# A Mamba-2 scan woven into matmul products: TensorE's instructions in traced order, the mask applied late, loads two steps ahead

## The chip, the cores and the metric

The kernel runs on one core of a Trainium2 chip. The metric is the device time of one launch in microseconds, as the median of the runs; a run is also profiled, and the profile gives every instruction of every engine with start and duration.

## What is computed

The reference is one decoder block: an RMSNorm, a wide projection `n @ w_in`, a Mamba-2 branch (SSD) and a gated linear attention branch (GLA) on parts of it, a gated merge, cross-attention to a short memory, and a SwiGLU feed-forward, all in float32 with 1024 tokens and 1024 features. The change lies in the SSD branch, which is, cut to what matters:

```python
xBC = silu(causal_dwconv(xBC, conv_w, conv_b))          # conv over tokens, then Silu
xs, Bm, Cm = split(xBC, [1024, 1024 + 2 * 128], axis=-1)
X = x_heads * dt[..., None]; a_cs = cumsum(dt * A)       # per chunk
CB = einsum('bclgn,bcsgn->bcgls', Cc, Bc)
y_diag = einsum('bcgls,bgrcls,bcsgrp->bclgrp', CB, segsum_exp(a), X)
states = einsum('bclgn,bgrcl,bclgrp->bcgrpn', Bc, exp(a_cs[..., -1:] - a_cs), X)
# state of a chunk = state before * exp(a_cs[..., -1]) + states
y_off = einsum('bclgn,bcgrpn,bgrcl->bclgrp', Cc, prev_state, exp(a_cs))
y = (y_diag + y_off + D * x_heads) * silu(z)
y = rmsnorm over each group's 512 features
```

There are 16 heads of 64 features in two groups, and a state of 128. The kernel uses chunks of 128 tokens, so there are 8 chunks x 2 groups = 16 items.

## The kernel before, in words

The projection is computed in units of 256 output columns. A unit (`Unit`, line 273) is one level of a seven-product scheme: its products B11, T2, T1, B21, T3, B22, T4 (this order is `SPACED`, line 40, and holds for a unit that runs alone) are each 12 matmuls of 128 x 128 by 128 x 512 into one PSUM bank. For each product, ScalarE makes the high part `whi` of the weights, VectorE the rest `wlo`, and VectorE or ScalarE evacuates the bank into `o`; GpSimd or VectorE makes the sums and differences of weights (`sa`, `raw`). These side instructions are traced with a priority 200 ahead of their place.

The kernel is written for a scheduler. The Python program traces instructions in one order; the scheduler then puts each engine's instructions in an order of its own, by priority and by when a model of the chip says that their inputs are ready. On the chip each engine runs its own list in that fixed order and waits on semaphores.

Ahead of the stage in question, six units (`xu`) project the channels of the convolution. `conv(u, unit)` (line 723) runs one unit behind: ScalarE starts a block `cv` of 128 channels, VectorE adds three taps, ScalarE applies Silu, and SP stores the block to `xbc_d` in DRAM. Unit 5 holds the rows of C (two blocks, one for each group). Its convolution is traced whole after the last unit's products and before the stage in question.

The stage in question then runs nine units (`ru`, `qk`, the first of `gs`), 63 products, and `run` (line 436) weaves the SSD steps between them: after each product it adds a rate to a counter, and for each whole number in it the generator `ssd_steps` is advanced to its next `yield`, with a priority of `PRIO` = 1000 ahead. Before the change the rate is 64/63, and what is left over is traced after the 63 products.

An item (class `SSD`, line 870) has these parts:

- `load`: SP loads the item's x channels and z gate (`xz`), B and C (`bc`), and a broadcast of the cumulated decay (`csb` from `cs_d`).
- `lay`: TensorE multiplies B and C (`bank<-bc`) and transposes B and the x channels into two banks; VectorE masks CB with a triangle (`cbm`), ScalarE copies B's transpose (`bt`), VectorE scales x by dt (`xd`).
- `decay`: ScalarE makes `e` (eight Relus with a bias, one Exp) and the Exp of `csb`; GpSimd makes `xc`; VectorE multiplies `csb` by C and `e` by the masked CB.
- `scan`: TensorE's 16 + 16 small products (`bank<-e,xd`, `bank<-csb,state`) and the state's products (`bank<-xc,bt`); GpSimd and VectorE update the state.
- `gate`: VectorE, GpSimd and ScalarE make `y` and the sum of its squares, `rd`.
- `stat`: a matmul sums `rd` over partitions, VectorE and GpSimd make the inverse root `rs`.
- `norm`: a matmul spreads `rs`, VectorE scales `y`, SP stores it to `ys_d`.

PSUM has four banks (`bank`) for these and four (`acc`) for the products. The SSD buffers (`xz` 3, `bc` 2, `csb` 2, `e` 2, `xc` 1) lie where the convolution's buffers lay.

Of the kernel before, what the change touches and what calls it, by code (L numbers as in the profile page):

```python
# [9 lines left out]
F32 = mybir.dt.float32  # L10
# [6 lines left out]
P = 128  # L17
# [11 lines left out]
CH = 128  # L29
NCH = TOK // CH  # L30
NH = 16
GH = 8
# [3 lines left out]
PRIO = 1000  # L36
# [42 lines left out]
def block_kernel(ctx: ExitStack, tc: tile.TileContext, t: dict, out: bass.AP):  # L79
    nc = tc.nc  # L80
    now = [0.0]
    PE, ACT, SP = Tensor(nc.tensor, now), nc.scalar, nc.sync
    DVE, POOL = Meter(nc.vector, now, 0.06, 1.04e-3), Meter(nc.gpsimd, now, 0.08, 2.25e-3)
# [6 lines left out]
    def pool(name, bufs=1, space=None, stack=None):  # L90
        kw = {"reuse_waits": "tile"} if space is None else {"space": space}
        return (stack or ctx).enter_context(tc.tile_pool(name=name, bufs=bufs, **kw))
# [6 lines left out]
    def dram(name, *shape):  # L99
        return dr.tile(list(shape), F32, name=name, tag=name)  # L100
# [4 lines left out]
    xbc_d = dram("xbc_d", 1536, TOK)  # L105
    sz_d = dram("sz_d", D, TOK)
# [18 lines left out]
    def bank(dt=F32):  # L125
        return ps.tile([P, 512], dt, name="bank", tag="bank", bufs=4)
# [3 lines left out]
    mul = lambda e, o, a, b: e.tensor_tensor(o, a, b, ALU.mult)  # L130
# [35 lines left out]
    triu = cp.tile([P, P], F32, name="triu")  # L166
# [106 lines left out]
    class Unit:  # L273
# [10 lines left out]
        def load(s):  # L284
            if s.raw is None:
                s.raw = slot(s.key, (P, 2 * s.kh, 256), name="raw")
                SP.dma_start(s.raw, s.W[s.row0:s.row0 + 256 * s.kh, s.c0:s.c0 + 256].rearrange("(k p) c -> p k c", p=P))
# [124 lines left out]
    def group(units, B, then=(), nxt=None, frm=6, products=7):  # L412


        for u in units:
            u.load()
        then = list(then)
        many = len(units)
        for n, name in enumerate((CHAIN if many > 1 else SPACED)[:products]):
            for x, u in enumerate(units):  # L420
                u.step(name, B)
                if many > 1:
                    B.upto((n + 1) * B.kh - (-(x + 1) * B.kh // many))
                if n == 6 and nxt:
                    nxt.upto((x + 1) * nxt.kh // many)
                if n >= frm and then:
                    then.pop(0).load()
                while len(posts) > lag[0]:
                    settle()
                    if n < 4:  # L430
                        break
                yield
        for u in then:
            u.load()

    def run(main, *rest, prio=0):

        owed = [0.0] * len(rest)
        for _ in main:
            for i, (g, rate) in enumerate(rest):  # L440
                owed[i] += rate
                while owed[i] >= 1.0:
                    owed[i] -= 1.0
                    with tc.high_priority(offset=prio):
                        next(g, None)
# [5 lines left out]
    def drain(g):  # L451
        for _ in g:
            pass

    def singles(units, B, then=()):

        for u, nxt in zip(units, list(units[1:]) + [None]):
            yield from group([u], B, [nxt] if nxt else then)

    def store_rows(dst, func=None):  # L460

        def mk(base):
            def post(i, j, ap):
                if func is not None:
                    ACT.activation(ap, ap, func)
                SP.dma_start(dst[base + i * P:base + (i + 1) * P, half(j)], ap)
            return post
        return mk

    def w_in_units(c0, n, mk):  # L470
        return [Unit(t["w_in"], 0, c0 + 256 * u, post=mk(256 * u)) for u in range(n)]
# [64 lines left out]
    for k in range(NB):  # L536
        p = bank()
# [73 lines left out]
    B = Operands(hb, 4)  # L611
# [230 lines left out]
    ru = w_in_units(R0, 4, store_rows(sr_d))  # L842
    qk = w_in_units(Q0, 2, store_rows(q_d)) + w_in_units(K0, 2, store_rows(k_d))
    gs = w_in_units(GS0, 4, store_rows(gs_d))
# [18 lines left out]
    sp_ = pool("ssd", 1, stack=st3)  # L863
# [6 lines left out]
    class SSD:  # L870
# [8 lines left out]
        def load(s):  # L879
            g, tk = s.g, s.tk  # L880
            s.L = sp_.tile([P, 8, CH], F32, name="xz", tag="xz", bufs=3)
            SP.dma_start(s.L[:, 0:4], xbc_d[g * 512:(g + 1) * 512, tk].rearrange("(k p) s -> p k s", p=P))
            s.BC = sp_.tile([P, 2, CH], F32, name="bc", tag="bc", bufs=2)
            for i in range(2):
                r0 = 1024 + i * 256 + g * P
                SP.dma_start(s.BC[:, i], xbc_d[r0:r0 + P, tk])
            s.csb = sp_.tile([P, GH, CH], F32, name="csb", tag="csb", bufs=2)
            SP.dma_start(s.csb.rearrange("p h s -> p (h s)"),
                         cs_d[s.i0:s.i0 + GH, :].rearrange("h s -> (h s)").partition_broadcast(P))
            SP.dma_start(s.L[:, 4:8], sz_d[g * 512:(g + 1) * 512, tk].rearrange("(k p) s -> p k s", p=P))  # L890

        def lay(s):
            p = bank()
            PE.matmul(p[:, :P], s.BC[:, 0], s.BC[:, 1], start=True, stop=True)
            PE.transpose(p[:, P:2 * P], s.BC[:, 0], ident)
            s.cbm = sp_.tile([P, CH], F32, name="cbm", tag="cbm", bufs=2)
            mul(DVE, s.cbm, p[:, :P], triu)
            s.bt = sp_.tile([P, P], F32, name="bt", tag="bt", bufs=2)
            ACT.activation(s.bt, p[:, P:2 * P], AF.Copy)
            p = bank()  # L900
            for k in range(4):
                PE.transpose(p[:, k * P:(k + 1) * P], s.L[:, k], ident)
            s.xd = sp_.tile([P, GH, 64], F32, name="xd", tag="xd", bufs=2)
            mul(DVE, s.xd, p.rearrange("p (h d) -> p h d", d=64), s.heads(dt_h, 64))

        def decay(s):
            s.e = sp_.tile([P, GH, CH], F32, name="e", tag="e", bufs=2)
            for h in range(GH):
                ACT.activation(s.e[:, h], s.csb[:, h], AF.Relu, bias=cs[:, s.i0 + h:s.i0 + h + 1], scale=-1.0)  # L909
            ACT.activation(s.e, s.e, AF.Exp, scale=-1.0)  # L910
            ACT.activation(s.csb, s.csb, AF.Exp)
            s.xc = sp_.tile([P, GH, 64], F32, name="xc", tag="xc", bufs=1)
            mul(POOL, s.xc, s.xd, s.heads(dec, 64))
            mul(DVE, s.csb, s.csb, s.BC[:, 1].unsqueeze(1).to_broadcast([P, GH, CH]))
            mul(DVE, s.e, s.e, s.cbm.unsqueeze(1).to_broadcast([P, GH, CH]))

        def scan(s):
            st = state[s.g]
# [37 lines left out]

    def ssd_steps():
        it = [SSD(c, g) for c in range(NCH) for g in range(2)]
        it[0].load()
        yield  # L960
        it[0].lay()
        yield
        it[0].decay()
        yield
        for i in range(len(it) + 1):
            z = it[i - 1] if i else None
            a = it[i] if i < len(it) else None
            b = it[i + 1] if i + 1 < len(it) else None
            if b:
                b.load()  # L970
            if a:
                a.scan()
            yield
            if z:
                z.stat()
            if b:
                b.lay()
            yield
            if a:
                a.gate()  # L980
            yield
            if z:
                z.norm()
            if b:
                b.decay()
            yield

    ssd = ssd_steps()
    run(singles(ru + qk + gs[:1], B, gs[1:2]), (ssd, 16 * 4 / 63), prio=PRIO)
    drain(ssd)  # L990
    st3.close()

# [426 lines left out]
    for n in range(len(at) + 2):  # L1419
        a = at[n] if n < len(at) else None  # L1420
        b = at[n - 1] if 0 < n <= len(at) else None
        z = at[n - 2] if n > 1 else None
# [59 lines left out]
    B = Operands(b_xo, 4, order=("B11", "T1", "B21", "B22", "T2", "T3", "T4"))  # L1482
# [147 lines left out]
    for x, (n, k, kn) in enumerate(todo):  # L1630
        name = CHAIN[n]
# [58 lines left out]
```

## Time and profile before

| what | value |
|---|---|
| median of 3 runs (1959.33 to 1963.98) | 1959.69 us |
| the profiled execution: time, span of the trace | 1964.03 us, 1962.3 us |
| mean granted clock of TensorE | 0.996 |
| DMA | 317.98 MB, 162 GB/s over the span |
| `wlo<-raw,whi` on VectorE, stage of SSD and GLA | x75, mean 881 ns |
| `o<-acc,o` on VectorE, the same | x74, mean 683 ns |
| `cbm<-bank,triu` on VectorE | x16, median 275 ns |
| `rs<-bank` on VectorE; `rs<-rs,mhalf` on GpSimd | median 145 ns; mean 1041 ns |
| ScalarE's idle time before `e<-csb,cs`, until `csb` landed | 17.4 us, 11 times |

The profile calls the engines PE (TensorE's matmuls), PEld (its weight loads), DVE (VectorE), ACT (ScalarE), POOL (GpSimd) and SP (the queue that issues the DMAs). Matmuls overlap in the records: one lasts 389 ns in the mean, though in a full stream one starts every 0.227 us, so busy time alone hides short waits. `L51` is the line of a helper that records every matmul and `L73` that of one which records every VectorE and GpSimd instruction, so groups are told apart by the names of their tiles: `acc<-T2h,whi` is a matmul of a product, `bank<-bc` the first of an item's `lay`.

### The profile page before, as it was taken

Reading aid. Unit: us, or ns where it says so; the run is one execution under the profiler, and the core shown is the slowest. Engines: PE = TensorE matmul, PEld = TensorE weight load, DVE = VectorE, ACT = ScalarE, POOL = GpSimd, SP = SyncE. Lnnn points to the kernel's source line nnn. Section 1 sums busy time; section 2 is a strip of 40 time slices with the busy share of each in tenths; the row PEclk is TensorE's granted clock in tenths of the full one; section 3 lists DMA queues with packets and bytes.
Section 4 is the critical chain, followed back from the end, with each engine's and each line's share of the span. In section 5 each row is a group of like instructions: output and inputs, shape, how many; then the busy total and the mean of one; then the engine's idle time right before and its main releaser. Section 6 shows DMA issues by size and latency. Waiting matters only on the chain.

```text
span 1962.3 us, 26274 instructions
## 1 busy us (share of the span) xinstructions
PE 1921.4 (98%) x9772; PEld 1614.9 (82%) x9772; DVE 1315.5 (67%) x1851; ACT 848.2 (43%) x1492; POOL 595.7 (30%) x442
## 2 busy tenths in 40 slices
PE   8899999999999999999999999999999999999998
PEld 7898787878788888888888888878888888878887
DVE  6866779789886655565544246676777777774565
ACT  8434564465552554642223235453333333353243
POOL 1012334355553212113342000037444544320002
PEclk9999999999999999999999999999999999999999
DMA  9333373456544653997684101442242233176463
GB/s 314 140 120 100 124 285 108 149 182 197 167 155 134 204 161 104 355 365 260 244 290 152 47 22 44 145 134 81 92 133 99 81 110 132 62 276 209 160 225 120
DMA packets 238244, 317.98 MB, mean 162 GB/s; under 512 B 16907, under 2 KB 156405, under 8 KB 238117
## 3 DMA queue, kind: packets, MB, share of 16 engines
q1 hardware_dynamic: 238116, 316.31, 47.5%
q8 instruction: 77, 1.26, 0.3%
q14 instruction: 51, 0.41, 0.1%
HBM read 215.27 MB, written 100.99 MB: 161 GB/s over the span
## 4 chain that ended last, share of the span: by engine, by line
PE 76%; DVE 11%; issue 3%; DMA 3%; ACT 3%; POOL 2%; SPq 1%; POOLq 0%; DVEq 0%; ACTq 0%
PE acc L51 67%; PE bank L51 9%; DVE wlo L73 3%; DVE cv L73 2%; DVE o L73 2%; PE bank L55 1%; DMA csb<-cs_d 1%; DMA xt<-in_x_dram 1%; ACT e L909 1%; DVE hs L73 1%; DMA raw<-in_w_in_dram 1%; DMA fr<-act_d 1%; DVE fs L73 1%; POOL y L73 1%; POOL sa L73 0%
## 5 line engine op out<-in xcount | busy, mean ns | idle before, releaser
L51 PE MATMUL acc<-hl,wd 128*128 128x512 f32 x1920 | 438.7, 389 | 0.0
L51 PEld LDWEIGHTS acc<-hl,wd 128*128 128x128 f32 x1920 | 360.1, 188 | 74.3
L73 DVE TENSOR_TENSOR wlo<-raw,whi 128x512 fp32r<-128x512 f32 x272 | 245.4, 907 | 89.5 <-ACT whi L221 87.4
L221 ACT ACTIVATE whi<-raw 128x512 fp32r<-128x512 f32 x272 | 169.6, 628 | 238.5 <-PE acc L51 211.0
L73 DVE TENSOR_TENSOR o<-acc,o 128x512 f32<-128x512 f32 (+1 forms) x256 | 172.6, 676 | 115.8 <-PE acc L51 105.0
L73 POOL TENSOR_TENSOR sa<-raw 128x512 f32<-128x512 f32 x47 | 75.5, 1607 | 306.6 <-DMA raw<-in_w_ffn_in_dram 227.1
L51 PE MATMUL acc<-fs 128*128 128x512 f32 (+1 forms) x792 | 157.6, 358 | 2.2 <-ACT o L1585 2.0
L51 PEld LDWEIGHTS acc<-fs 128*128 128x128 f32 x792 | 131.8, 190 | 23.7 <-ACT o L1585 2.4
L73 POOL TENSOR_TENSOR raw<-raw,sa 128x512 f32<-128x512 f32 x48 | 68.7, 1431 | 242.8 <-DVE wlo L73 231.9
L221 ACT ACTIVATE fs<-fr 128x1024 fp32r<-128x1024 f32 (+1 forms) x84 | 80.0, 984 | 114.8 <-PE acc L51 40.5
L73 DVE TENSOR_TENSOR fs<-fr,fs 128x1024 fp32r<-128x1024 f32 (+1 forms) x84 | 99.7, 1218 | 40.5 <-ACT fs L221 40.1
L221 ACT ACTIVATE whi<-sa 128x512 fp32r<-128x512 f32 x96 | 60.0, 626 | 104.5 <-PE acc L51 101.4
L73 DVE TENSOR_TENSOR wlo<-sa,whi 128x512 fp32r<-128x512 f32 x96 | 82.9, 865 | 16.1 <-ACT whi L221 16.1
L73 DVE TENSOR_TENSOR wd<-raw,wd 128x1024 fp32r<-128x1024 f32 x40 | 53.3, 1334 | 48.5 <-ACT wd L221 48.4
L221 ACT ACTIVATE wd<-raw 128x1024 fp32r<-128x1024 f32 x40 | 42.2, 1059 | 96.0 <-PE acc L51 89.4
L73 POOL TENSOR_TENSOR raw<-raw 128x512 f32<-128x512 f32 x48 | 82.5, 1718 | 3.0 <-DVE sa L73 2.8
L51 PE MATMUL acc<-T4h,whi 128*128 128x512 f32 x192 | 75.9, 396 | 1.8 <-DVE o L73 1.8
L51 PE MATMUL acc<-B22h,wlo 128*128 128x512 f32 x192 | 76.2, 397 | 1.3 <-DVE wlo L73 1.3
L51 PE MATMUL acc<-B21h,whi 128*128 128x512 f32 x192 | 75.3, 392 | 1.4 <-ACT o L350 1.4
L51 PE MATMUL acc<-B21h,wlo 128*128 128x512 f32 x192 | 75.5, 393 | 0.4 <-DVE wlo L73 0.4
L51 PE MATMUL acc<-T3h,wlo 128*128 128x512 f32 x192 | 75.8, 395 | 0.0
L51 PE MATMUL acc<-B22h,whi 128*128 128x512 f32 x192 | 75.6, 394 | 0.0
(386 smaller groups left out, 4651.9 us busy)
## 6 DMA issues: line engine op xcount, KB each, us to landing
raw<-in_w_in_dram SPq DMA_DIRECT2D x26, 1024.0 KB, 5.7
raw<-in_w_ffn_in_dram SPq DMA_DIRECT2D x22, 1024.0 KB, 8.0
act_d<-o SPq DMA_DIRECT2D x77, 256.0 KB, 2.1
fr<-act_d SPq DMA_DIRECT2D x35, 512.0 KB, 6.0
pre<-in_w_ffn_out_dram SPq DMA_DIRECT2D x11, 1024.0 KB
fr<-down_d SPq DMA_DIRECT2D x20, 512.0 KB, 4.9
down_d<-pre SPq DMA_DIRECT2D x33, 256.0 KB, 3.5
raw<-in_w_xkv_dram SPq DMA_DIRECT2D x8, 1024.0 KB, 7.6
```

What stands on the lines that cost most here:

```text
L51: return s.e.matmul(o, x, y, **kw)
L55: return s.e.transpose(o, x, i)
L73: return f(*a, **kw)
L221: ACT.activation(hi, src, AF.Copy)
L909: ACT.activation(s.e[:, h], s.csb[:, h], AF.Relu, bias=cs[:, s.i0 + h:s.i0 + h + 1], scale=-1.0)
```

## The change

TensorE's instructions of the whole stage are put in the order in which they are traced, instead of the scheduler's order. The steps are dealt out anew, 74/63 to a product, so that all of them lie within the 63 products: with numbers for the steps of item i, step 1 has the `norm` of item i - 2 and the `scan` of item i; step 2 the `load` of item i + 2, the `stat` of item i - 1, the `lay` of item i + 1 and the `gate` of item i; step 3 the `decay` of item i + 1 and the load of `csb` for item i + 2; step 4 nothing. Ahead of them come the loads of two items after the first product, `lay` of item 0 after the second, its `decay` after the third, and its `scan` after the fourth. The mask is multiplied into CB in `decay`, with its result in the third quarter of CB's own bank, and the multiplication of `e` reads it there. B and C come with one DMA instead of two, into three buffers instead of two.

```diff
-            s.BC = sp_.tile([P, 2, CH], F32, name="bc", tag="bc", bufs=2)
-            for i in range(2):
-                r0 = 1024 + i * 256 + g * P
-                SP.dma_start(s.BC[:, i], xbc_d[r0:r0 + P, tk])
+            s.BC = sp_.tile([P, 2, CH], F32, name="bc", tag="bc", bufs=3)
+            SP.dma_start(s.BC, xbc_d[1024:1536, tk].rearrange("(i g p) s -> g p i s", g=2, p=P)[g])
+            SP.dma_start(s.L[:, 4:8], sz_d[g * 512:(g + 1) * 512, tk].rearrange("(k p) s -> p k s", p=P))
+
+        def load_cs(s):
             s.csb = sp_.tile([P, GH, CH], F32, name="csb", tag="csb", bufs=2)
             SP.dma_start(s.csb.rearrange("p h s -> p (h s)"), ...)
-            SP.dma_start(s.L[:, 4:8], sz_d[g * 512:(g + 1) * 512, tk].rearrange("(k p) s -> p k s", p=P))
...
-            p = bank()
+            p = s.p = bank()
...
-            s.cbm = sp_.tile([P, CH], F32, name="cbm", tag="cbm", bufs=2)
-            mul(DVE, s.cbm, p[:, :P], triu)
...
-            mul(DVE, s.e, s.e, s.cbm.unsqueeze(1).to_broadcast([P, GH, CH]))
+            cbm = s.p[:, 2 * P:3 * P]
+            mul(DVE, cbm, s.p[:, :P], triu)
+            mul(DVE, s.e, s.e, cbm.unsqueeze(1).to_broadcast([P, GH, CH]))
...
-        it[0].load()
+        n = len(it)
+        for s in it[:2]:
+            s.load()
+            s.load_cs()
         yield
         it[0].lay()
         yield
         it[0].decay()
         yield
-        for i in range(len(it) + 1):
-            z = it[i - 1] if i else None
-            a = it[i] if i < len(it) else None
-            b = it[i + 1] if i + 1 < len(it) else None
-            if b:
-                b.load()
+        for i in range(n + 2):
+            y, z, a, b, c = (it[k] if 0 <= k < n else None for k in range(i - 2, i + 3))
+            if y:
+                y.norm()
             if a:
                 a.scan()
             yield
+            if c:
+                c.load()
             if z:
                 z.stat()
             if b:
                 b.lay()
-            yield
             if a:
                 a.gate()
             yield
-            if z:
-                z.norm()
             if b:
                 b.decay()
-            yield
+            if c:
+                c.load_cs()
+            yield
+            if i < n:
+                yield
 
     ssd = ssd_steps()
-    run(singles(ru + qk + gs[:1], B, gs[1:2]), (ssd, 16 * 4 / 63), prio=PRIO)
+    with tc.manual_schedule(engines={mybir.EngineType.PE}):
+        run(singles(ru + qk + gs[:1], B, gs[1:2]), (ssd, 74 / 63), prio=PRIO)
     drain(ssd)
```

## The prediction

> **What bounds the kernel now.** I read the page first, then a table by stage, then the waits of TensorE inside the SSD stage.
>
> ```profile
> PE 1921.4 (98%) x9772; PEld 1614.9 (82%) x9772; DVE 1315.5 (67%) x1851; ACT 848.2 (43%) x1492; POOL 595.7 (30%) x442
> ```
> ```profile
> 380.00:593.00 213.00, 208.00 (x1320) 169.06 (x1320) 181.28 (x287) 117.36 (x257) 114.47 (x90) 1.00 0.58 178
> 593.00:787.00 194.00, 194.00 (x967) 163.96 (x967) 112.59 (x224) 83.30 (x198) 48.63 (x41) 1.00 0.49 153
> ```
>
> The columns of the second fence are the window, its length, busy time of PE, PEld, DVE, ACT and POOL, granted clock, DMA share, GB/s. TensorE bounds the kernel. The change touches only the stage of about 213 us in the first row, where TensorE is idle for 213.00 - 208.00 = 5.0 us; after it, TensorE has no idle time at all, so nothing can be gained there by releasing work sooner. VectorE comes second, at 181.28 / 213 = 85%.
>
> So the change is worth what TensorE's waits in this stage cost, less what new waits cost. The waits of TensorE and of its weight loads, by releaser (us in total, times, longest), in 380 to 630 us:
>
> ```profile
> PE bank L51 <- POOL rs L73: 2.8, 4, 1.0
> PE bank L51 <- DVE y L73: 1.4, 3, 0.6
> ```
> ```profile
> PEld bank L51 <- POOL rs L73: 5.3, 6, 1.4
> PEld bank L51 <- DVE y L73: 1.7, 3, 0.7
> PEld bank L51 <- DVE wlo L73: 1.1, 3, 0.4
> PEld acc L51 <- DVE wlo L73: 1.1, 2, 0.6
> PEld bank L51 <- DVE o L73: 0.7, 2, 0.4
> PEld acc L51 <- ACT whi L221: 0.6, 1, 0.6
> ```
>
> A weight load waits while the last matmul is still counted as busy, so the second table is the fuller measure: 5.3 + 1.7 + 1.1 + 1.1 + 0.7 + 0.6 = 10.5 us is the most that better placed instructions can win; 2.8 + 1.4 = 4.2 us, counted as idle, is the least if all go. The large one is `rs`: the norm's broadcast matmul stands two steps behind the statistic that it needs.
>
> **The change, part by part.** *Distances (gain).* In the new loop `norm` stands three steps behind `stat`. A product is 12 matmuls:
>
> ```profile
> 787.00 300.57 PE acc L51 x1326
> ```
>
> This line of the chain of waits gives 300.57 / 1326 = 0.227 us a matmul, 2.72 us a product. There are 74/63 steps to a product, so three steps are two or three products, at least 5.4 us, against a VectorE instruction of 0.15 us and a GpSimd power of about 1 us (the table ahead of this part) with the queues before them. The `rs` and `y` waits should go. The order also makes new ones. Between `lay` and the `scan` that needs it lie two products (5.4 us) for 6 of 15 items and three for the rest. In that time VectorE must do:
>
> ```profile
> L73 DVE TENSOR_TENSOR e<-e,cbm 128x1024 f32<-128x1024 f32 x16 | 31.1, 1941 | 2.1 <-ACT e L910 1.6
> L73 DVE TENSOR_TENSOR csb<-csb,bc 128x1024 f32<-128x1024 f32 x16 | 21.4, 1335 | 2.5 <-ACT csb L911 2.3
> L73 DVE TENSOR_TENSOR xd<-bank,dtv 128x512 f32<-128x512 f32 x16 | 10.9, 680 | 0.0
> L73 DVE SCALAR_TENSOR_TENSOR y<-xz,dcol,bank 128x128 f32<-128x128 f32 x64 | 17.8, 337 | 0.8 <-PE bank L51 0.8
> ```
>
> That is 1.94 + 1.34 + 0.68 + 4 x 0.34 = 5.3 us and the mask's 0.28 us (from the table), if all of it falls there. Part of it doesn't: `csb` needs no `lay`, and the four gate operations can run while the scan's successor product streams. I price this at 0 to 1 us for each of the six short items and take 3.0 us. Relief: 10.5 - 3.0 = **-7.5 us** (between -10.5 and -4.2 + 6 = +1.8).
>
> *CB masked in its bank.* The mask's product now lies in PSUM, and the large multiplication of `e` reads one operand there instead of two in SBUF.
>
> ```profile
> L73 DVE TENSOR_TENSOR e<-e,cbm x16: 1224/2134/2267, 394.8 to 586.6; 128x1024 f32<-128x1024 f32 x16
> ```
> ```profile
> L73 DVE TENSOR_TENSOR xd<-bank,dtv x16: 677/679/684, 392.5 to 591.0; 128x512 f32<-128x512 f32 x16
> ```
>
> Minimum, median and maximum: two SBUF operands spread from 1224 to 2134 ns, an operand in PSUM holds 680 ns for half the size. So I expect 1.2 to 1.4 us instead of 1.94; the bounds are 1.2 and 2.1. The 16 x 0.7 = 11 us that VectorE saves are off the path, and already lie in the relief above. The bank is held longer; four banks for six in an item leave the second bank of `lay` waiting only where `scan` and `lay` fall together, within the 0 to 6 us.
>
> *Loads two steps ahead; four DMAs become three for an item, and `csb` goes last.* ScalarE is idle before `e<-csb,cs` for 17.4 us in this stage (the same table), none of which appears among TensorE's waits: nothing. SP's queue is passed by the same bytes; a load that waits for its buffer holds the stores behind it, as it does now.
>
> *TensorE in program order (loss), at the entry.* This is the largest term. The SSD steps are woven in from the first product of `ru[0]`: loads after B11, `lay(0)` after T2. But `lay(0)` reads what the last convolution stores, and that convolution runs while `ru[0]` does. The timeline at the entry, engine by engine (start, us, instruction):
>
> ```profile
> 371.44 0.39 PE L51 MATMUL acc<-T1h,whi 128*128 128x512 f32 x1
> ...
> 388.71 0.39 PE L51 MATMUL bank<-bc 128*128 128x128 f32 x2
> ```
> ```profile
> 369.13 2.47 DVE L73 SCALAR_TENSOR_TENSOR cv<-o,cols,cv 128x1023 f32<-128x1023 f32 x2
> 371.52 0.69 DVE L73 TENSOR_TENSOR wlo<-raw,whi 128x512 fp32r<-128x512 f32 x1
> 372.12 0.68 DVE L73 TENSOR_TENSOR o<-acc,o 128x512 f32<-128x512 f32 x1
> 372.72 2.00 DVE L73 SCALAR_TENSOR_TENSOR cv<-o,cols,cv 128x1022 f32<-128x1022 f32 x1
> ...
> 376.35 0.68 DVE L73 TENSOR_TENSOR o<-acc,o 128x512 f32<-128x512 f32 x1
> 376.95 1.71 DVE L73 SCALAR_TENSOR_TENSOR cv<-o,cols,cv 128x1023 f32<-128x1023 f32 x1
> ```
> ```profile
> 378.69 1.06 ACT L737 ACTIVATE cv<-cv 128x1024 f32<-128x1024 f32 x1 [0.71 <-DVE cv L73]
> ```
> ```profile
> 371.59 0.32 SPq L738 DMA_DIRECT2D xbc_d<-cv  x1
> ...
> 379.77 0.32 SPq L738 DMA_DIRECT2D xbc_d<-cv  x1
> 381.59 0.32 SPq L466 DMA_DIRECT2D sr_d<-o  x1
> 382.09 0.37 SPq L882 DMA_DIRECT2D xz<-xbc_d  x1
> 382.82 0.79 SPq L886 DMA_DIRECT2D bc<-xbc_d  x2
> ```
> ```profile
> DMA to landing us min/median/max: 2.7/3.7/4.6
> ```
>
> T2 of `ru[0]` ends where T1 begins, at 371.44. In the old order `lay(0)` runs at 388.71, after seven products, and costs nothing, since TensorE has those products to do. In program order it stands at 371.44, ahead of T1, and everything behind it on TensorE waits too. When can it run? The last block's taps end at 376.95 + 1.71 = 378.66 in the trace; the evacuation of 0.68 us at 376.35 belongs to T1 and falls away: 378.0. The Silu (1.06 us) ends at 379.1 and the store goes out. The trace has 2.32 us from that store to the first SSD load, with a store between that would not be there; the bare issue is 0.32; I take 1.3. So the first load is at 380.4, `bc` behind it at 380.8, landed 3.7 us later (the last fence is of `bc`): 384.5. The wait is 384.5 - 371.44 = **+13.0 us**. Low: the last two taps follow at 372.80 without a gap, at 1.28 us, then 1.06, 0.32, 0.37 and a landing of 2.7: 379.8, so 8.4. High: the load as traced, at 382.09 + 0.37, and 4.6: 387.1, so 15.6.
>
> *The clock after that pause.*
>
> ```profile
> 50.00:60.00 10.00, 5.32 (x30) 5.33 (x31) 10.00 (x18) 5.22 (x10) 0.00 (x0) 0.66 1.07 391
> 1760.00:1765.00 5.00, 4.43 (x13) 3.50 (x14) 2.52 (x3) 3.02 (x7) 0.00 (x0) 0.68 0.55 206
> ```
>
> Where TensorE paused before, the granted clock fell: a mean of 0.68 over 5 us costs (1 - 0.68) x 5 = **+1.6 us** (0 if the drop ends in the pause; 3.4 by the first row). The Trainium skill ("TensorE: Matmul & The Clock Gate", Part 1) has the clock halved after an idle window of about 3.4 us and whole again after a busy one as long, which would be an estimated 1.7 us here; the second row's pause was shorter than 3.4 us and its clock fell all the same, so in that the trace is stricter than the page.
>
> *First scan.* `scan(0)` stands two products behind `lay(0)`:
>
> ```profile
> 388.93 2.45 ACT L909 ACTIVATE e<-csb,cs 128x128 f32<-128x128 f32 x8 [2.34 <-DMA csb<-cs_d]
> ```
> ```profile
> 396.67 1.21 DVE L73 TENSOR_TENSOR csb<-csb,bc 128x1024 f32<-128x1024 f32 x1
> ```
>
> From the landing of `csb` to its product took 397.88 - 388.93 = 8.95 us; `csb` lands about 2 us after `bc`, and TensorE has 0.8 + 2 x 2.72 + 1.6 = 7.8 us of work: a wait of at most 3 us, and less with VectorE freed: **+2.0 us**.
>
> Sum: 13.0 + 1.6 + 2.0 - 7.5 = **+9.1 us**. The profiled execution took 1964.03 us, 4.3 above the median of 1959.69; I add the difference to the median: **1968.8 us**. About 0.3% (5.9 us) is what a measurement of this kernel can tell from no change.
>
> **Rivals.** *A, faster: no wait at the entry.* If the order kept on TensorE is not the traced one, or the first `lay` slips behind the products, the terms of the entry vanish: -7.5 us, 1952.2. Against it:
>
> ```profile
> 526.35 0.49 PE L51 MATMUL bank<-ident,rs 128*128 128x128 f32 x2 [1.02 <-POOL rs L73]
> 526.59 0.48 PE L51 MATMUL acc<-B22h,whi 128*128 128x512 f32 x1
> ```
>
> When the norm's matmul waited for `rs`, the next product's matmul did not pass it. The Trainium skill ("TensorE: Matmul & The Clock Gate", Part 3, The mechanism) says so too: weight loads are pulled ahead, matmuls start in strict order. A gain over 5.9 us needs an entry under 2 us even with the whole relief. Chance 0.13.
>
> *B, no change.* If the loads need only the first block of the last convolution (its store at 371.59), `bc` lands at 371.59 + 2.32 + 0.37 + 3.7 = 378.0 and the wait is 6.5 us: +2.6 us, 1962.3. Against it: in the trace, with SP idle and a priority of 1000, the loads still stand behind the store at 379.77. Chance 0.17.
>
> *C, slower still: VectorE becomes the bound of every item.* If the multiplication of `e` stays at 2.1 us or the gate is put ahead of it, each `scan` finds `e` late. This decides as soon as the work above (5.6 us) with two products' splits and evacuations (2 x 1.56, by 0.88 and 0.68 us in the table) is not over within two products; at 1 us for each of 15 items it is 15 instead of 3: +21 us, 1981. The fall of VectorE's share speaks against. Chance 0.10.
>
> **How the numbers follow.** The sum above has 0.60; its own range is 1958 to 1977. Slower: four fifths of it (0.48), all of C, 0.02 of B: 0.60. Faster: 0.12 of A and 0.01 of B: 0.13. The rest, 0.27, is within 0.3%. The range 1954 to 1981 leaves out A's 0.12 and some 0.06 above.
>
> **What would show it.** Right: a pause of TensorE of 8 to 16 us just before the first `bank<-bc`, near 371 us of the span, released by `bc`'s DMA; a clock of 0.5 for about 3 us behind it; `rs` gone from TensorE's waits; `e` at 1.2 to 1.4 us; no seven products ahead of the first `lay`. Wrong: no such pause (then A, and the time is below before), or the waits of `bank<-e,xd` on VectorE summing over 10 us (then C).

## The result, and the profile after

The changed kernel took 1984.76 us in the median of 4 runs (1983.97 to 1986.05), the kernel before 1961.24 us in 4 runs (1959.33 to 1963.98): a ratio of 1.0123, 95% interval 1.0111 to 1.0135. It is slower by 23.5 us, where 9.1 were forecast. The span of the profiled execution grew from 1962.3 to 1983.5 us, by 21.2.

The page of the profile after gives the busy time of each engine:

```profile
span 1983.5 us, 26255 instructions
PE 1924.5 (97%) x9772; PEld 1624.8 (82%) x9772; DVE 1290.0 (65%) x1851; ACT 847.3 (43%) x1492; POOL 587.9 (30%) x442
```

TensorE's work is the same to the instruction (9772), and VectorE has 1290.0 us of work instead of 1315.5. Of the table by stage, the row of the stage in question (window, length, busy time of PE, PEld, DVE, ACT, POOL, granted clock, DMA share, GB/s):

```profile
380.00:593.00 213.00, 197.63 (x1225) 165.65 (x1226) 142.11 (x258) 109.41 (x240) 93.90 (x81) 0.94 0.55 170
```

The loss lies in this row: TensorE idles 15.4 us there (and 8 more ahead of it, from 371.7 us on) instead of 5.0, at a clock of 0.94 instead of 1.00, and 95 fewer matmuls fall into the same window. From 593 to 787 us TensorE is busy for 193.58 of 194.00 us, nearly as before. What TensorE's matmuls waited for from 360 to 650 us (total, times, longest):

```profile
PE bank L51 <- DMA bc<-xbc_d: 12.9, 1, 12.9
PE bank L51 <- DVE e L73: 3.6, 3, 1.9
PE acc L51 <- DVE o L73: 2.6, 2, 1.8
PE bank L55 <- issue: 1.6, 1, 1.6
PE bank L51 <- issue: 1.3, 1, 1.3
PE bank L51 <- DVE y L73: 1.1, 1, 1.1
```

Two more, of 0.4 and 0.2 us, follow; the one of 0.2, on `wlo` at 361 us, is in the kernel before too. `rs`, the largest releaser before, is gone. In its place stand one wait of 12.9 us and nine short ones, on `e`, on evacuations (`o`) and on banks. The entry on the timeline (start, us, instruction), first TensorE, then SP:

```profile
371.69 0.39 PE L51 MATMUL acc<-T2h,wlo 128*128 128x512 f32 x1
385.02 0.80 PE L51 MATMUL bank<-bc 128*128 128x128 f32 x2 [12.94 <-DMA bc<-xbc_d]
...
387.11 0.63 PE L51 MATMUL acc<-T1l,whi 128*128 128x512 f32 x1
387.53 0.63 PE L51 MATMUL acc<-T1h,wlo 128*128 128x512 f32 x1
```
```profile
372.07 8.47 SPq L738 DMA_DIRECT2D xbc_d<-cv  x2
381.19 0.78 SPq L884 DMA_DIRECT2D bc<-xbc_d  x1
```

The first `lay` stands behind T2, and its load behind the second convolution block's store. T1 behind it streams at one matmul in 0.42 us, nearly twice the usual 0.227. The clock, in the four stretches where it fell (same columns as above):

```profile
377.00:390.00 13.00, 4.98 (x15) 4.30 (x16) 3.03 (x3) 2.30 (x6) 5.13 (x5) 0.50 0.65 194
396.00:401.00 5.00, 4.06 (x33) 3.69 (x33) 2.90 (x6) 4.54 (x9) 0.66 (x1) 0.66 0.09 26
458.00:465.00 7.00, 5.67 (x16) 4.63 (x17) 4.55 (x12) 3.16 (x10) 3.91 (x4) 0.52 0.69 206
557.00:561.00 4.00, 4.00 (x35) 3.55 (x34) 4.00 (x8) 0.67 (x2) 0.77 (x1) 0.57 0.31 104
```

What the half clock cost is estimated as the busy time in each row times what was not granted: 4.98 x 0.50 + 4.06 x 0.34 + 5.67 x 0.48 + 4.00 x 0.43 = 2.5 + 1.4 + 2.7 + 1.7 = 8.3 us. Around the start of each stand waits of TensorE: the 12.9 us at the first, and these at the second (the first `scan`) and at the third (a `scan` and a `lay` in one place, where the `lay` waits for banks):

```profile
395.16 0.44 PE L51 MATMUL bank<-e,xd 128*64 128x128 f32 x4 [1.26 <-DVE e L73]
396.94 0.70 PE L51 MATMUL bank<-csb,state 128*64 128x128 f32 x4 [1.34 <-issue]
...
457.17 0.49 PE L51 MATMUL bank<-bc 128*128 128x128 f32 x2 [1.14 <-DVE y L73]
...
459.33 1.08 PE L55 MATMUL bank<-ident,xz 128*128 128x128 f32 x4 [1.56 <-issue]
```

Ahead of the fourth it is one of the two-product items, here first on TensorE, then on ScalarE, then on VectorE:

```profile
548.23 0.47 PE L51 MATMUL bank<-bc 128*128 128x128 f32 x2
...
556.84 0.44 PE L51 MATMUL bank<-e,xd 128*64 128x128 f32 x4 [1.92 <-DVE e L73]
```
```profile
550.61 0.63 ACT L940 ACTIVATE sq<-y 128x512 f32<-128x512 f32 x1 [7.29 <-POOL y L73]
551.14 2.44 ACT L907 ACTIVATE e<-csb,cs 128x128 f32<-128x128 f32 x8
553.49 0.61 ACT L221 ACTIVATE whi<-raw 128x512 fp32r<-128x512 f32 x1
```
```profile
554.14 0.69 DVE L73 TENSOR_TENSOR wlo<-raw,whi 128x512 fp32r<-128x512 f32 x1 [1.51 <-ACT whi L221]
554.77 0.30 DVE L73 TENSOR_TENSOR bank<-bank,triu 128x128 f32<-128x128 f32 x1
...
555.58 1.21 DVE L73 TENSOR_TENSOR e<-e,bank 128x1024 f32<-128x1024 f32 x1
```

`lay` began at 548.23, two products behind it TensorE was at the `scan`, and `e` was finished at 556.79: 8.6 us after the `lay`. TensorE waited 1.92 us, and the row of 557 to 561 us above, right behind it, has a clock of 0.57. The rows of the other two engines show what was late: the mask and the multiplication of `e` stand on VectorE behind a split `wlo`, which waited 1.51 us for ScalarE's `whi`; that stood behind the eight Relus of the next item's `decay`, and these behind the gate's `sq`, for which ScalarE had waited 7.29 us on GpSimd's `y`. The item's own Exp had ended at 541.33, well ahead of its `lay`.

The account: 12.9 (the load) + 10.6 (the other new waits: 3.6 + 2.6 + 1.6 + 1.3 + 1.1 + 0.4) + 8.3 (the clock) = 31.8 us lost. To set against it, the first matmul of the next stage, which is the same one by number in both kernels, before and after:

```profile
807.25 1.07 PE L51 MATMUL acc<-hl,wd 128*128 128x512 f32 x4
```
```profile
830.30 1.07 PE L51 MATMUL acc<-hl,wd 128*128 128x512 f32 x4
```

From the last matmul of T2 (371.21 before, 371.69 after) to it went 436.0 us before and 458.6 after: the stretch grew by 22.6 us. (The span grew by 21.2, because behind it the execution before lost some 2 us at 1760 us, in a pause of 2.03 us and the lowered clock that the prediction shows, and the one after lost less there: 1.60 us, at full clock.) So about 9 us came back. The old waits of TensorE, counted in the same way, were 5.0 us in all; the other 4 us are a difference and are read from no row.

### The profile page after: what moved, and what is told of

It reads as the page before. It is cut to its first block, busy times and chain, and to the rows that moved or that the text cites. A ratio compares the mean times of both kernels' runs of the same rounds, so it can differ in the third digit from the quotient of the medians.

```text
span 1983.5 us, 26255 instructions
## 1 busy us (share of the span) xinstructions
PE 1924.5 (97%) x9772; PEld 1624.8 (82%) x9772; DVE 1290.0 (65%) x1851; ACT 847.3 (43%) x1492; POOL 587.9 (30%) x442
## 4 chain that ended last, share of the span: by engine, by line
PE 78%; DVE 10%; DMA 3%; ACT 3%; issue 3%; POOL 2%; SPq 1%; POOLq 0%; DVEq 0%; ACTq 0%
PE acc L51 67%; PE bank L51 9%; DVE wlo L73 2%; DVE cv L73 2%; DVE o L73 1%; PE bank L55 1%; DMA raw<-in_w_in_dram 1%; DMA xt<-in_x_dram 1%; ACT e L907 1%; DVE hs L73 1%; DVE fs L73 1%; DMA fr<-act_d 1%; DMA csb<-cs_d 1%; POOL sa L73 1%; ACT whi L221 0%
## 5 line engine op out<-in xcount | busy, mean ns | idle before, releaser
L73 DVE TENSOR_TENSOR wlo<-raw,whi 128x512 fp32r<-128x512 f32 x272 | 238.8, 883 | 102.7 <-ACT whi L221 102.5
L51 PE MATMUL acc<-T3h,whi 128*128 128x512 f32 x192 | 76.6, 399 | 0.0
L51 PE MATMUL acc<-B11h,whi 128*128 128x512 f32 x192 | 76.3, 397 | 0.0
L51 PE MATMUL acc<-T3l,whi 128*128 128x512 f32 x192 | 76.1, 396 | 0.0
```

The costliest lines, as they stand in the source:

```text
L51: return s.e.matmul(o, x, y, **kw)
L73: return f(*a, **kw)
```

## The experiments

The theories. The entry: the traced order puts the first `lay` two products into `ru[0]`, 13 us ahead of its data. The distance: behind the entry `e` comes late, since six items have only two products between `lay` and `scan`. Its rivals: late `e` is due to the doubled steps (`scan` and `lay` in one place), to the gate standing ahead of `decay`, or to the traced order as such. Where a text below numbers them, 2a is the distance and 2b the gate's place.

**e1_entry_late.** Six empty steps ahead of the first `lay`:

```diff
+        for _ in range(6):
+            yield
         it[0].lay()
```

> The changed kernel with six empty steps between the first loads and the first lay: lay(0) then stands after the seventh product and not after the second; all distances within the loop are kept, and the last steps fall behind the 63 products. Theory 1 (the loss is the entry, and what the entry drags behind it): the pause of 13.3 us before the first bank<-bc goes, with the half clock after it (about 4 us) and the waits of the first scan (2.9 us): about 20 us less than the changed kernel, 1963 to 1968, within 7 us of before. Theory 2 (the order itself costs at every item, rival C): the pause goes too, but the time stays above 1972, since waits of the later items grow in its place.

Measured: 1970.4 us, 1.0038 (1.0025 to 1.0051) of before at 1962.25. The pause at 371 us is gone and the time falls by 14.4 us, though not to before. The largest wait that is left, from 360 to 650 us:

```profile
PE bank L51 <- DVE e L73: 9.2, 6, 4.7
```

The first `scan`, still two products behind its `lay`, accounts for 4.7 of these 9.2 us. It waits 1.1 us more for `csb`'s product, and half clock follows it at once (0.57 from 395 to 403 us, with TensorE busy for 5.32 us: about 2.3 us). That is 8.1 us, about what e1 is still above before. So the place of the first `lay` is the largest part, and the first `scan` is the next.

**e2_free_order.** The changed kernel without the traced order; steps, mask and loads stay:

```diff
-    with tc.manual_schedule(engines={mybir.EngineType.PE}):
-        run(singles(ru + qk + gs[:1], B, gs[1:2]), (ssd, 74 / 63), prio=PRIO)
+    run(singles(ru + qk + gs[:1], B, gs[1:2]), (ssd, 74 / 63), prio=PRIO)
```

> The changed kernel without the traced order on TensorE: new steps, mask in the bank, new loads, but the scheduler orders TensorE's instructions. Theory 1: no pause at the entry and no waits at scan and lay placed back to back; the waits of the norm mostly gone by its larger distance: 1953 to 1962. Theory 2 (the new steps or the mask in PSUM cost by themselves): over 1970.

Measured: 1961.95 us, 0.9999 (0.9989 to 1.0009). The whole loss comes with the traced order; the other parts taken together, with the scheduler free to place them, are worth nothing that this measurement can tell. The trace has no wait on `rs` left, of matmuls or of weight loads, from 360 to 650 us; its largest is one of 3.7 us on `e`.

**e3_order_alone.** The kernel before with the traced order as its only edit (its steps stay):

```diff
-    run(singles(ru + qk + gs[:1], B, gs[1:2]), (ssd, 16 * 4 / 63), prio=PRIO)
+    with tc.manual_schedule(engines={mybir.EngineType.PE}):
+        run(singles(ru + qk + gs[:1], B, gs[1:2]), (ssd, 16 * 4 / 63), prio=PRIO)
```

> The kernel before with the traced order on TensorE and nothing else: old steps, old distances. Theory 1: the same entry, lay(0) after the second product, so a pause of 12 to 14 us with its clock loss, and in addition the norm's wait for rs at many items, since two steps at 64/63 are two products: 1980 to 1995, at or above the changed kernel. If the new distances and not the order made the loss (theory 2), this one stays within 6 us of before.

Measured: 1971.43 us, 1.0045 (1.003 to 1.006). Its weight loads' waits, from 360 to 650 us:

```profile
PEld bank L51 <- DMA bc<-xbc_d: 13.3, 1, 13.3
```

The entry's pause is there, as it should be. The time expected, 1980 to 1995, is not: the loss is 9.2 us, not the 23.5 of the change with the same pause. The waits on `rs` that were expected are missing: with the old steps in traced order, TensorE waits for almost nothing once the entry is past (its matmuls 1.3 us). In the old steps `lay` stands three products ahead of its `scan`, and `e` was finished 2.2 to 5.9 us behind `lay` at all items but the first. So the traced order takes the waits on `rs` away without the new distances, as e2's new distances do without the traced order: either is enough.

**e4_no_double.** The changed kernel with 1 step a product, and the fourth, empty step in every other item only, so that `scan` and `lay` never fall in one place; eight items then have two products between `lay` and `scan` instead of six:

```diff
-            if i < n:
+            if i < n and i % 2:
                 yield
...
-        run(..., (ssd, 74 / 63), prio=PRIO)
+        run(..., (ssd, 1.0), prio=PRIO)
```

> The changed kernel with one step after each product, the empty step only in every other item, so that scan and lay of different items never fall into the same place (in the changed kernel they do for three items of sixteen); entry as in the changed kernel. Theory: the waits at these three places (4.4, 0.9 and 1.2 us beyond the others, clock included) go: 4 to 8 us less than the changed kernel, 1977 to 1981. If it is VectorE's work between lay and scan that waits (rival C), there is no gain, because two products between them become more frequent (8 items of 15, not 6): 1984 or above.

Measured: 1986.2 us, 1.0117 (1.0102 to 1.0132), as slow as the change. Matmuls from 360 to 650 us:

```profile
PE bank L51 <- DVE e L73: 7.4, 6, 1.8
```

Behind the first `scan`, `e` is late at five of the two-product items (465, 494, 524, 553 and 583 us), where the change has two. The waits on `o` are gone and those for banks are smaller. The run changes two things at once, no doubled steps and more short items, and they level out: the doubled steps are not the only cause, but that they cost nothing isn't shown.

**e5_old_steps_late.** e3 with a late entry: `lay` of item 0 behind the seventh product (as in e1), its `scan` four steps behind `decay`, and what does not fit behind the 63 products:

```diff
-        yield
+        for _ in range(6):
+            yield
         it[0].lay()
         yield
         it[0].decay()
-        yield
+        for _ in range(4):
+            yield
```

> The kernel before with the traced order on TensorE and a late entry, nothing else: old steps and distances, lay(0) after the seventh product, scan(0) after the twelfth, what is left over behind the 63 products. The run of the order alone lost 13.3 us before the first lay and 3 to 5 us more in the half clock and the first scan behind it, and showed no other wait of TensorE. Theory 1 (the order is a gain of about 11 us, and the entry took it away): 1951 to 1957, ratio 0.995 to 0.998. Theory 2 (the order gains nothing and only the entry differs): 1960 to 1964. If the steps behind the 63 products cost more than before: above 1966.

Measured: 1971.8 us, 1.0046 (1.0033 to 1.006) of before at 1962.41. In the stage TensorE runs nearly unbroken, better than before (208.00):

```profile
380.00:593.00 213.00, 211.55 (x1294) 174.93 (x1295) 161.99 (x269) 110.86 (x240) 102.16 (x82) 1.00 0.57 180
```

But the last steps are late (the last norm's matmul stands at 640.8 us instead of 629.3), and where the next stage's first dense matmul needs its weights, they are not ready: ScalarE makes the first `wd` at 811.4 us instead of 802.5. The wait in 790 to 850 us, and the window with the clock:

```profile
PEld acc L51 <- ACT wd L221: 7.6, 2, 7.3
```
```profile
810.00:820.00 10.00, 7.52 (x21) 5.93 (x22) 2.45 (x2) 5.90 (x9) 0.00 (x0) 0.58 0.88 310
```

What the entry no longer costs is paid at the end, since a late entry and 3.9 products an item do not fit in 63 products. The links between the late steps and the late weights were not followed; that the wait is absent in e9 and e12, where all fits, speaks for it.

**e6_new_steps_late.** The changed kernel with the same late entry and 64/63 steps to a product, so that all items have three products between `lay` and `scan` (the late entry's lines are those of e5):

```diff
-            if i < n:
-                yield
+            yield
...
-        run(..., (ssd, 74 / 63), prio=PRIO)
+        run(..., (ssd, 64 / 63), prio=PRIO)
```

> The changed kernel with the same late entry and one step to a product (64/63, the empty step in every item), so that three products lie between every lay and its scan as in the old steps. Theory 2a (the two-product distance is what made e late at its scan): no waits for e, within 3 us of the run with the old steps and late entry. Theory 2b (the new place of gate, with its squares ahead of the decay's Relus on ScalarE, makes e late whatever the distance): e still ends 5 to 9 us behind its lay, and what three products (9.4 us) do not cover waits: 3 to 8 us above it.

Measured: 1971.46 us, 1.0047 (1.0031 to 1.0063). No wait for `e` is left in 360 to 650 us; the one at the end is (weight loads wait 6.7 us for `wd`). `e` is still finished only 5.0 to 9.9 us behind its `lay`, and three products cover it. With them the new steps are as good as the old.

**e7_gate_last.** e1 with the `gate` moved from the second step to the fourth, behind `decay`:

```diff
-            if a:
-                a.gate()
             yield
             if b:
                 b.decay()
...
             if i < n:
+                a.gate()
                 yield
```

> The first run (changed kernel, late entry, 1970.4 us) with one thing moved: gate stands in the empty fourth step, behind the next item's decay, and not in the second. Distances stay at two or three products. Theory 2b: the squares no longer stand ahead of the Relus on ScalarE, e ends 3 to 6 us behind its lay and not 5 to 9, the waits at the scans (0.8 to 2.0 us each, some 6 us with the doubles) go: 1962 to 1966. Theory 2a: unchanged, 1968 to 1972.

Measured: 1971.72 us, 1.0044 (1.0031 to 1.0058), beside 1.0038 for e1. The waits for `e` from 360 to 650 us are no fewer: 10.5 us in 7, against 9.2 in 6. The gate's place in the trace is not what makes `e` late. (That doesn't clear the gate's `sq` in ScalarE's queue: that queue's order is the scheduler's.)

**e8_old_steps_late_mask.** e5 with the mask's product left in its bank:

```diff
-            mul(DVE, s.e, s.e, s.cbm.unsqueeze(1).to_broadcast([P, GH, CH]))
+            cbm = s.p[:, 2 * P:3 * P]
+            mul(DVE, cbm, s.p[:, :P], triu)
+            mul(DVE, s.e, s.e, cbm.unsqueeze(1).to_broadcast([P, GH, CH]))
```

> The run with the old steps, the order and the late entry, with one thing more: the mask multiplied late in CB's bank. VectorE's multiplication of e then takes 1.2 us and not 1.9 to 2.1 (16 x 0.7 = 11 us less on VectorE), but waits for the mask behind it. If VectorE's share matters for TensorE's waits: 2 to 4 us below that run. If not: the same within 2 us.

Measured: 1967.77 us, 1.003 (1.0019 to 1.004), 4 us below e5 beside the same runs of before, though the two intervals overlap. The wait at the end is still there (`wd`, 6.2 us). So VectorE's shorter work is worth something in the traced order too.

**e9_three_products.** Three steps for an item, one to a product, in traced order, with the mask in its bank and the late entry; all of it fits in 63 products. Step 1 has `norm` of i - 2 and `scan` of i, step 2 `stat` of i - 1 and `lay` of i + 1, step 3 `gate` of i and `decay` of i + 1. From the old steps, without the mask's and the entry's lines:

```diff
+            if y:
+                y.norm()
             if a:
                 a.scan()
             yield
             if z:
                 z.stat()
             if b:
                 b.lay()
             yield
             if a:
                 a.gate()
-            yield
-            if z:
-                z.norm()
             if b:
                 b.decay()
             yield
```

> Old steps with the traced order, the mask late in its bank, the late entry (lay(0) after the seventh product, scan(0) after the twelfth), and an item in three products: scan with the norm of two items before, then stat and lay, then gate and decay, one step after each product, so that all is done within the 63 products. The runs with the late entry that went over the end paid 6 to 7 us and a half clock where the first matmul behind the stage waits for its weights (near 805 us). Theory (order gains about 10 us, entry and end each take it away when they are pushed): no pause at the entry beyond 1.5 us, no wait near 800 us, no half clock: 1950 to 1957, ratio 0.995 to 0.998. Rival (TensorE in order gains nothing, the runs only move a fixed loss about): 1960 to 1966. If two products between lay and scan are too few here too: waits for e at the scans, 1962 to 1970.

Measured: 1969.07 us, 1.0036 (1.0023 to 1.0048) of before at 1961.93: not the gain that was expected first, but its last case. No wait at the end; but only two products between `lay` and `scan`, now at every item:

```profile
PE bank L51 <- DVE e L73: 10.9, 9, 2.2
```

**e10_three_products_free.** e9 without the traced order:

```diff
-    with tc.manual_schedule(engines={mybir.EngineType.PE}):
-        run(..., (ssd, 1.0), prio=PRIO)
+    run(..., (ssd, 1.0), prio=PRIO)
```

> The run before this one without the traced order: the scheduler orders TensorE's instructions, everything else equal. Theory: 5 to 10 us more than with the order, 1958 to 1964. Rival: equal within 2 us, so that the steps and the entry make the gain and the order none.

Measured: 1961.24 us, 0.9996 (0.9987 to 1.0005). In the free order the same steps lose nothing, against the expectation that the order gains 5 to 10 us. The trace shows why: in traced order 24 matmuls of products, two products, stand between a `lay` and its `scan`; in the free order the scheduler put 34 to 44 there at 14 of the 15 items behind the first, and no `scan` waits for `e`.

**e11_three_products_early.** e9 with the change's early entry:

```diff
-        for _ in range(6):
-            yield
+        yield
         it[0].lay()
         yield
         it[0].decay()
-        for _ in range(4):
-            yield
+        yield
```

> The first run of this call with the entry of the change: loads, lay(0), decay and scan(0) after the first four products. It prices the entry alone in a loop without other waits. Theory: a pause of 13 us before the first bank<-bc, some 2.5 us by the half clock behind it and 2 to 3 us at the first scan: 15 to 20 us more than the first run. If the entry costs only the pause: 12 to 14 us more.

Measured: 1984.55 us, 1.0113 (1.01 to 1.0127). Against e9, one edit, the early entry costs 15.5 us (1984.55 - 1969.07). Most of it is the pause:

```profile
PEld bank L51 <- DMA bc<-xbc_d: 13.1, 1, 13.1
```

**e12_lay_with_scan.** e9 with `lay` of i + 1 moved one step ahead, directly behind `scan` of i, so that three products lie between a `lay` and its `scan`. The gate and the `decay` thereby stand one product behind the `scan` instead of two, the loads go one item further ahead and the norm one step further back (without the loop's own line and the line of `y, z, a, b, c`):

```diff
+        it[1].load()
...
-            if b:
-                b.load()
-            if y:
-                y.norm()
             if a:
                 a.scan()
-            yield
-            if z:
-                z.stat()
             if b:
                 b.lay()
+            if i == n + 1:
+                y.norm()
             yield
+            if z:
+                z.stat()
             if a:
                 a.gate()
             if b:
                 b.decay()
+            if c:
+                c.load()
             yield
+            if y and i <= n:
+                y.norm()
+            yield
```

> The three-product steps in traced order with the late entry (1969.07, with two products between lay and scan), but lay(i+1) directly behind scan(i), so that three products lie between a lay and its scan, all steps within the 63 products. If the two-product distance is what costs the traced order (e late at every item), the waits for e fall below 2 us in all, there is no wait at 805 us, and the time is 1957 to 1962, level with before or a little below. If the order costs by itself, it stays at 1966 to 1971. If scan and lay back to back run out of banks, waits of TensorE on y or xd of 1 us or more stand at every item and the time is above 1972.

Measured: 1961.73 us, 0.9996 (0.9987 to 1.0005) of before at 1961.77. All of TensorE's waits from 360 to 650 us:

```profile
PE bank L51 <- DVE y L73: 1.8, 3, 0.9
PE bank L51 <- DMA bc<-xbc_d: 1.4, 1, 1.4
PE acc L51 <- DVE rs L73: 0.6, 1, 0.6
PE acc L51 <- DVE wlo L73: 0.4, 2, 0.2
```

No wait for `e`, none at the end. One item of each, first e9 (`lay`, `scan`), then e12 (`lay`, `scan`, and `e`):

```profile
501.30 0.47 PE L51 MATMUL bank<-bc 128*128 128x128 f32 x2
...
510.20 0.44 PE L51 MATMUL bank<-e,xd 128*64 128x128 f32 x4 [2.20 <-DVE e L73]
```
```profile
480.49 0.38 PE L51 MATMUL bank<-bc 128*128 128x128 f32 x2
...
490.15 0.44 PE L51 MATMUL bank<-e,xd 128*64 128x128 f32 x4
```
```profile
486.44 1.21 DVE L73 TENSOR_TENSOR e<-e,bank 128x1024 f32<-128x1024 f32 x1
```

In this item of e12 `e` is finished at 487.65, 7.2 us after its `lay`: later than two products allow (in e9 TensorE reaches the `scan` 6.6 us after the `lay` where nothing waits), but within three (9.5 us). With the order kept, 7.3 us are gone against e9 (1969.07, where before had 1961.93). So the traced order as such costs nothing here.

But the edit moved more than the distance. In e9 VectorE waits 2.4 to 3.2 us for ScalarE's `whi` ahead of the mask at all six items where TensorE then waits 0.9 us or more for `e`; in e12, and in e3, no such wait of even 0.9 us stands there at any item behind the first. `e` comes sooner for it: 2.9 to 7.3 us behind `lay` in e12, 5.2 to 8.8 in e9. At these times of e12 two products would have left some 2.5 us of waits (an estimate: what goes beyond 6.6 us at six items), not 10.9. How the 7.3 us divide between the distance and the shorter queue is not shown.

**e13_mask_alone.** The kernel before with the mask in its bank as its only edit (the diff of e8), in the free order:

> Before, with the mask's product left in its bank as the only edit (no traced order, old steps, old loads). If the mask's gain of 4 us in the traced order came from VectorE reaching e sooner, the free order has only its 5.0 us of idle time to win from: 1957 to 1961 beside 1961, ratio 0.998 to 1.000, with e at 1.2 us. If the scheduler deals the order out anew and loses, up to 1966.

Measured: 1958.86 us in 11 runs, 0.9987 (0.9978 to 0.9996) of before at 1961.77. This is the one version faster than before, by 0.13%, less than what the prediction called measurable; the interval excludes no change only narrowly. From 380 to 593 us VectorE has 170.18 us of work instead of 181.28, and TensorE is busy for 209.97 us: it idles 3.0 us instead of 5.0.

## Why the prediction missed

The sign was right, the size was not: +23.5 us between the medians against +9.1. Two steps failed, each by more than 6 us: the clock, +8.3 instead of +1.6, and the relief net of new waits, about -1.2 instead of -7.5. The other two terms held (12.9 for the pause and 2.6 for the first `scan`, against 13.0 and 2.0). By the prediction's own steps:

- *The pause at the entry:* right to 0.1 us: 12.9 against 13.0, released by `bc`'s DMA behind the second block's store. Rivals A and B fell with it.
- *The clock:* mis-sized, 8.3 us against 1.6 (0 to 3.4). Behind the pause alone it cost 2.5, not 1.6, because the clock was still at half for some 5 us after TensorE had started again. And the prediction priced it once, though it fell again at three of the new waits, one of 1.9 us and two pairs of 1.1 to 1.6 us; these stretches cost 5.8 us. The prediction had the warning in its own second row of a lowered clock, which follows a pause that it says is shorter than 3.4 us (2.03 us in the trace).
- *First scan:* about right: 1.3 + 1.3 = 2.6 us against 2.0.
- *The relief net of new waits:* the stretch grew by 22.6 us, and 22.6 - 12.9 - 8.3 - 2.6 leaves -1.2 us, a difference, where -7.5 stood. New waits beside the first `scan` came to 8.0 us, not 3.0. Those on `e` were not the error: 2.4 us, at two of the six short items. The prediction priced `e` alone and put at nothing what TensorE waits for VectorE's evacuations `o` (2.6 us); the place where `lay` and `scan` fell together, which it had inside its 0 to 6, cost 2.7. And what the old waits were worth was taken from the weight loads (10.5 us), where the matmuls' own waits were 5.0. The waits on `rs` did go, as forecast, but the kernels without them and without the pause gained little: e2 is level with before, and so is e12 with 4.2 us of waits left. That speaks for the smaller measure and doesn't prove it.
- *The late `e`:* the prediction summed VectorE's 5.3 us for an item and held them against 5.4. In the item shown that sum was not what bound: VectorE itself waited, through `wlo`, `whi` and ScalarE's queue, on the gate's `y`, and `e` was finished 8.6 us after `lay`. The chain had to be read across the engines, from end to end. In the changed kernel this cost little beyond the first `scan` and the clock behind it; in e4 and e9, with more short items, it cost more (waits of 7.4 and 10.9 us).
- *The mask in its bank:* right for the instruction: `e` takes 1.21 us (1.2 to 1.4 forecast, 1.94 before). The prediction called the time that VectorE saves off the path and counted it inside the relief; by itself it gained 2.9 us (e13).
- *Rival C* (`e` late at every item, 1981, chance 0.10) is nearer to the time than the forecast, but by luck more than by what happened. `e` multiplied at 1.21 us, so its first condition did not hold, and e7 speaks against its second, the gate's place. The waits of `bank<-e,xd` summed to 3.6 us, not over 10.

What is shown: that the entry costs 15.5 us, by e11 against e9; that the rest of the change, taken together, costs nothing in the free order, by e2; that the traced order with the steps of e12 costs nothing; and that three products cover a late `e`, by e6. What is open: why `e` comes 5 to 9 us after `lay` at most items of the change, and 2 to 6 us after it with the old steps (e3). The waits of VectorE for `whi` go with it in the traces, but no run took them away by themselves. What made the evacuations late at 496 and 526 us is open too.

## What to carry to other kernels

When one engine is put in traced order, price each distance by the time from a step's first input to its last output across all engines, read end to end from the timeline, not by the sum of work on the busiest of them. Look at the first and the last item by themselves: the first must stand behind its data, and what is moved back there must still fit ahead of the next stage. Ask of every engine's queue which new wait it can hand on to TensorE, evacuations included, and not only of the tile that the change is about. And price every new wait of about 2 us on TensorE with the clock that it may halve behind it.

## What the runs showed of the hardware

The granted clock halved behind short waits: of 1.92 us up to 556.84 us in the changed kernel (then 0.57 over 4 us), and of 2.10 us up to 416.17 us in e9, where the window behind it has 0.66:

```profile
416.00:421.00 5.00, 4.83 (x38) 4.13 (x39) 3.58 (x9) 0.95 (x2) 2.49 (x3) 0.66 0.95 306
```

Not each such wait did it. In the same run the longer wait of 2.20 us up to 510.20 us, in the row shown with e12, left the clock whole:

```profile
508.00:516.00 8.00, 5.80 (x51) 5.05 (x51) 6.62 (x13) 3.30 (x6) 2.84 (x3) 1.00 0.74 219
```

The Trainium skill ("TensorE: Matmul & The Clock Gate", Part 1) has the clock halved after an idle window of about 3.4 us that runs free of the kernel. These rows fit that it depends on where a pause falls, since its length alone doesn't decide, and disagree that it takes 3.4 us of idleness: 1.92 us sufficed.

An operand in PSUM shortened the multiplication of 128 x 1024 elements from 1941 to 1210 ns in the mean, with the mask's place as the only edit (e13). The gain is in the spread: single ones took 1224 to 2267 ns with both operands in SBUF, and 1202 to 1221 with one in PSUM. Its line among the groups, 380 to 593 us (busy, mean ns):

```profile
L73 DVE TENSOR_TENSOR e<-e,bank 128x1024 f32<-128x1024 f32 x16 | 19.4, 1210 | 0.1
```
